# A transformer layer's feed-forward network in parts of 8, 8 and 6 blocks, the down projection of two parts wholly in seven products

## The chip, the cores and the metric

The kernel runs on one core of one Trainium2 chip. The metric is the device time of one execution in microseconds (us), from runs of the same built kernel. The core's engines are named as in the profile: PE is the tensor engine, DVE the vector engine, ACT the scalar engine, POOL GpSimd, SP the engine that here issues most transfers. Each takes its instructions in the order in which the program lists them; they meet at semaphores.

## What is computed

Two layers work on 512 tokens of width 1024, in float32. Each layer mixes the tokens (attention, convolution, neighbourhood attention, merged by gates), then applies a feed-forward network, then a gated embedding. The change concerns the feed-forward network:

```
h = rmsnorm(x, norm_ffn[i])
x = x + (jax.nn.silu(h @ w_ffn_gate[i]) * (h @ w_ffn_up[i])) @ w_ffn_down[i]
```

The inner width is 2816, so 22 blocks of 128 (`NFB`). "Gate" and "up" give a block of middles, 128 x 512 (inner features by tokens); "down" multiplies all 22 blocks into 8 outputs of 128 x 512.

## The kernel before, in words

**Numbers as pairs.** Every operand of PE is split into a rounded high part and a rest (`split`, line 169): ACT copies the high part (line 150), DVE subtracts it (`tt`, line 164). A product of two operands is then three matmuls: high by high, high by low, low by high.

**Seven products.** Where two blocks of weights and two blocks of tokens form a 2 by 2 arrangement, the kernel computes the four results from seven block products in place of eight, as Strassen and Winograd do. The operands of the seven are sums: of weights (s1 to s4, built by accumulating transfers of POOL and by DVE) and of activations (t1 to t4). A product's moving side is 256 tokens wide.

**Three parts.** `ffn` (line 1244) walks the 22 blocks in three parts (`PARTS`): blocks 0 to 7, 8 to 14 and 15 to 21. For each block, `seven` (line 1129) multiplies the gate and up weights by the normalised tokens in seven products of 12 matmuls; DVE and ACT combine the results, apply silu and the product of gate and up, and split the middle block (`rest`). `rest` of a block is called in the next block, after its third product, by `flush`; after the last block of a part it is called at once. After each part, the down projection of that part's blocks runs:

- Parts one and two use `seven_down` (line 1030), called for p = 0 to 3, each for a pair of outputs (2p, 2p+1). Six blocks, paired as (0,1), (2,3), (4,5), go through the seven products R0, R1, T0, T1, A0, A1, C0. Each takes three chunks k, one for each pair of blocks, so nine matmuls of 128 x 256. The blocks that are left (`late`: 6 and 7 in part one, 14 in part two) are multiplied whole, each by two outputs (steps M and N, lines 1085 to 1087), three matmuls of 128 x 512 a time. The result goes to DRAM (`xa`).
- Part three uses ordinary products: `pair` for outputs 0 and 1, `gemm` for the rest, 7 blocks x 3 matmuls of 128 x 512 (lines 187 to 189) an output. During its blocks, `x[m]` is loaded from `xa[0]` and `xa[1]` is added by accumulating transfers of POOL.

**Sums of middles.** When a pair of middle blocks is ready, `middles` (line 1002) forms t1 to t4: u (t1 and t3 together, 512 columns), w (t2 and t4, 256 columns each), and splits each into high and low. The splits are put off to the `rest` of the next block (`parted`, `part_sums`); for the pair (12,13) the split of t2 comes at once. In an even block that takes part in the seven products only the first 256 columns are split, since its second half enters the products through sums alone.

**Order.** PE's order is that of the code (`manual_schedule`). The order on ACT, DVE and the queues is decided by a scheduler with priorities; work on weights is put ahead (`high_priority`), and `behind` pins one instruction behind another.

## Time and profile before

| what | us |
|---|---|
| median of 3 runs | 1760.77 |
| the runs | 1759.83 to 1761.42 |
| the profiled execution | 1761.55 |
| its span, first to last instruction | 1759.8 |
| layer 1: blocks 0 to 7 end, part one's down projection starts | 573.67 |
| part two's blocks start | 614.87 |
| part two's down projection starts | 685.19 |
| part three's blocks start | 721.17 |
| part three's down projection, start and end | 791.45, 829.56 |

Times are counted from the first instruction. A row of the timeline gives start, duration, engine, line, operation, output and inputs, shape. Rows of PE start before the row ahead has ended, since matmuls are pipelined: the distance of two starts is what a matmul costs. The same holds in a small way on DVE and ACT: the distance of starts counts where an engine has no pause.

### The profile page before, as it was taken

The page shows a single profiled execution, that of the slowest core. Times are in us where ns is not written, and L with a number is a line of the kernel's source. Part 1 is how long each engine was busy: PE and PEld are TensorE (multiplying, and loading weights), DVE is VectorE, ACT ScalarE, POOL GpSimd, SP SyncE. Part 2 cuts the span into 40 slices and gives each one's busy share as a digit, 9 for nine tenths or more (in the row PEclk, how much of TensorE's full clock was granted, in tenths as well). Part 3 has the DMA queues.
Part 4 walks back from the last instruction along what each step waited for, and adds up shares of the span by engine and source line. Part 5 has one row for each costly group of instructions (what it writes and reads, how often), then busy time and mean ns, then how long its engine had stood idle before and what let it go on. Part 6 is the DMA issues. An engine that isn't in the chain of part 4 may idle for free.

```text
span 1759.8 us, 28716 instructions
## 1 busy us (share of the span) xinstructions
PE 1752.0 (100%) x10578; PEld 1565.5 (89%) x10578; DVE 1473.8 (84%) x2528; ACT 929.6 (53%) x1623; POOL 140.3 (8%) x162
## 2 busy tenths in 40 slices
PE   9999999999999999999999999999999999999998
PEld 7888888888899999998888888888888999999987
DVE  7967987998799889887777678889887997998776
ACT  5576545225576455554545655552356654555454
POOL 0000000000111111210000000000001121112100
PEclk9999999999999999999999999999999999999999
DMA  6576641334867777975446755423257667779642
GB/s 225 165 186 160 162 126 45 111 99 141 265 167 173 205 194 171 253 206 165 159 134 175 180 148 152 113 72 96 93 173 245 178 167 218 187 189 253 159 153 96
DMA packets 137901, 288.67 MB, mean 164 GB/s; under 512 B 17184, under 2 KB 38432, under 8 KB 137760
## 3 DMA queue, kind: packets, MB, share of 16 engines
q1 hardware_dynamic: 117456, 251.96, 46.6%
q0 software_dynamic: 19584, 33.56, 12.0%
q8 instruction: 83, 1.36, 0.3%
q10 hardware_dynamic: 720, 1.31, 0.2%
q14 instruction: 58, 0.48, 0.1%
HBM read 236.43 MB, written 19.92 MB: 146 GB/s over the span
## 4 chain that ended last, share of the span: by engine, by line
PE 92%; DVE 4%; ACT 2%; DMA 1%; issue 1%; SPq 0%; POOL 0%; ACTq 0%; POOLq 0%; DVEq 0%
PE ffn_mm L1174 4%; PE ffn_mm L1176 4%; PE ffn_mm L1175 4%; PE ffn_sc L1174 3%; PE ffn_sc L1176 3%; PE ffn_sc L1175 3%; PE mergea_mm L188 2%; PE mergea_mm L189 2%; PE mergea_mm L187 2%; PE gateb_mm L188 2%; PE gateb_mm L189 2%; PE gateb_mm L187 2%; PE wo_mm L187 2%; PE wo_mm L189 2%; PE wo_mm L188 2%; PE diff_sc L837 2%
## 5 line engine op out<-in xcount | busy, mean ns | idle before, releaser
L167 DVE SCALAR_TENSOR_TENSOR conv_z<-glu_z,pre_par,conv_z 128x512 f32<-128x512 f32 x240 | 179.4, 748 | 3.5
L1144 POOL DMA_DIRECT2D ffn_qk<-w_fu x88 | 77.8, 973 | 432.8 <-DMA ffn_qk<-w_fu 88.7
L164 DVE TENSOR_TENSOR ffn_wl<-ffn_wr,ffn_wh 128x1024 fp32r<-128x1024 f32 (+1 forms) x76 | 89.3, 1177 | 6.7 <-ACT ffn_wh L150 6.7
L150 ACT ACTIVATE ffn_wh<-ffn_qk 128x1024 fp32r<-128x1024 f32 (+1 forms) x60 | 62.7, 1045 | 51.8 <-PE ffn_mm L1087 14.6
L150 ACT ACTIVATE ffn_wh<-ffn_wr 128x1024 fp32r<-128x1024 f32 (+1 forms) x76 | 76.8, 1014 | 22.5 <-PE ffn_mm L188 12.0
L150 ACT ACTIVATE mergea_wh<-mergea_wr 128x1024 fp32r<-128x1024 f32 (+1 forms) x32 | 27.1, 846 | 96.8 <-PE mergea_mm L188 79.6
L164 DVE TENSOR_TENSOR ffn_wl<-ffn_qk,ffn_wh 128x1024 fp32r<-128x1024 f32 (+1 forms) x60 | 72.3, 1205 | 6.7 <-ACT ffn_wh L150 6.3
L150 ACT ACTIVATE ffn_kh<-ffn_r 128x512 fp32r<-128x512 f32 (+1 forms) x60 | 35.9, 599 | 42.0 <-PE ffn_mm L1175 19.9
L233 POOL TENSOR_TENSOR diff_rc<-diff_sm,pre_power 128x4 f32<-128x4 f32 x8 | 8.9, 1116 | 563.8 <-DVE diff_sm L167 505.3
L150 ACT ACTIVATE diff_a<-diff_sc,diff_s 128x512 f32<-128x512 f32 x32 | 22.0, 686 | 57.2 <-DVE diff_s L931 57.1
L150 ACT ACTIVATE natten_e<-natten_e,natten_s 128x192 f32<-128x192 f32 (+1 forms) x88 | 39.3, 473 | 24.0 <-DVE natten_s L735 20.7
L1174 PE MATMUL ffn_sc<-wo_h,ffn_wh 128*128 128x256 f32 x176 | 50.4, 286 | 0.2 <-ACT ffn_t L150 0.2
L1175 PE MATMUL ffn_mm<-wo_h,ffn_wh 128*128 128x256 f32 x176 | 49.8, 283 | 0.0
L1176 PE MATMUL ffn_mm<-wo_h,ffn_wl 128*128 128x256 f32 x176 | 49.8, 283 | 0.0
L1174 PE MATMUL ffn_mm<-wo_h,ffn_wh 128*128 128x256 f32 x176 | 49.8, 283 | 0.0
L1176 PE MATMUL ffn_sc<-wo_h,ffn_wl 128*128 128x256 f32 x176 | 49.8, 283 | 0.0
L1175 PE MATMUL ffn_sc<-wo_h,ffn_wh 128*128 128x256 f32 x176 | 49.8, 283 | 0.0
L164 DVE TENSOR_TENSOR diff_wl<-diff_wr,diff_wh 128x1024 fp32r<-128x1024 f32 x24 | 29.3, 1223 | 18.6 <-ACT diff_wh L150 13.6
L150 ACT ACTIVATE natten_wh<-natten_wr 128x1024 fp32r<-128x1024 f32 x24 | 25.4, 1059 | 36.7 <-issue 15.2
L931 DVE TENSOR_REDUCE diff_s<-diff_sc 128x1 f32<-128x512 f32 x64 | 42.0, 683 | 2.7 <-PE diff_sc L837 2.5
L164 DVE TENSOR_TENSOR natten_wl<-natten_wr,natten_wh 128x1024 fp32r<-128x1024 f32 x24 | 29.3, 1222 | 12.4 <-ACT natten_wh L150 10.4
L164 DVE TENSOR_TENSOR ffn_qk<-ffn_qk,ffn_r 128x512 f32<-128x512 f32 (+1 forms) x60 | 38.9, 648 | 0.0
(1082 smaller groups left out, 6979.5 us busy)
## 6 DMA issues: line engine op xcount, KB each, us to landing
ffn_qk<-w_fu POOLq DMA_DIRECT2D x88, 256.0 KB, 6.5
ffn_wr<-w_fg SPq DMA_DIRECT2D x44, 512.0 KB, 5.5
ffn_r<-w_fu SPq DMA_DIRECT2D x44, 256.0 KB, 4.6
ffn_qk<-w_fg SPq DMA_DIRECT2D x44, 256.0 KB, 4.8
ffn_qk<-w_fu SPq DMA_DIRECT2D x44, 256.0 KB, 5.2
...
```

The source lines that it names most:

```text
L150: i = self.nc.scalar.activation(out, in_, func, **kw)
L164: return self.nc.vector.tensor_tensor(out, a, b, op)
L167: return self.nc.vector.scalar_tensor_tensor(out, a, s, b, op0, op1)
L187: mm(out, wh, ah, start=first, stop=False, skip_group_check=onto)
L188: mm(out, wh, al, start=False, stop=False, skip_group_check=onto)
L189: mm(out, wl, ah, start=False, stop=last, skip_group_check=onto)
L837: self.nc.tensor.matmul(out, st4[:, u, qs], st[:, ks], start=n == 0, stop=n == 1)
L931: nc.vector.tensor_reduce(out=m[:, u:u + 1], in_=sc, op=ALU.max, axis=AX.X, negate=True)
L1144: nc.gpsimd.dma_start(q, wu[:, lo], accum_op=ALU.add)
L1174: mm(out, wh[:, c], bh, start=first and k == 0, stop=False, skip_group_check=True)
L1175: mm(out, wh[:, c], bl, start=False, stop=False, skip_group_check=True)
L1176: mm(out, wl[:, c], bh, start=False, stop=k == 3, skip_group_check=True)
```

## The change

- `PARTS` becomes 0 to 7, 8 to 15 and 16 to 21. In parts one and two all eight blocks go through the seven products (four chunks, `KW` of 512), steps M and N are gone, and `DOWN`, the order in which the weights of the down projection lie in DRAM, follows. Part three has six blocks an output.
- Blocks 6 and 7 (14 and 15) get sums too (`middles` with `last`): their splits are not put off, and come in the order t2, t1, t3, then t4. In block 6 (14) only 256 columns are split.
- For p = 0 the seven products run in two rounds: first chunks 0 to 2 of all seven, then chunk 3, which holds the last two blocks, in the order R0, A0, A1, T0, R1, T1, C0 (`ORDERS`). For p = 1 the order is R0, A0, T0, A1, R1, T1, C0, for p = 2 and 3 it is `STEPS`.
- On the queues: a call of `seven_down` loads two sums of 256 KB, one block of 512 KB and one of 256 KB through SP (before: sums of 192 KB and a remainder, a block of up to 512 KB, and 192 KB), and POOL adds two of 256 KB (before 192 KB). The loads of `x` from `xa` move one block later.
- Two orders are pinned: for p = 1 the high part of the sums s1, s2 behind t4's low part, and p = 0's first subtraction behind p = 1's sum s4.

The diff, cut to its core:

```diff
-PARTS = (range(0, 8), range(8, 15), range(15, 22))
+PARTS = (range(0, 8), range(8, 16), range(16, 22))
...
-KW = 3 * P
-DOWN = (0, 2, 4, 1, 3, 5, 6, 7, 8, 10, 12, 9, 11, 13, *range(14, NFB))
+KW = 4 * P
+ORDERS = {0: ("R0", "A0", "A1", "T0", "R1", "T1", "C0"), 1: ("R0", "A0", "T0", "A1", "R1", "T1", "C0")}
+STEPS = ("R0", "A0", "R1", "T1", "T0", "A1", "C0")
+DOWN = (*range(0, 8, 2), *range(1, 8, 2), *range(8, 16, 2), *range(9, 16, 2), *range(16, NFB))
 QUARTERS = (2, 4, 6)
 ORDER = (0, 2, 4, 6, 1, 3, 5, 7)
...
@@ -167,7 +169,7 @@
         return self.nc.vector.scalar_tensor_tensor(out, a, s, b, op0, op1)
 
     def split(self, hi, lo, src):
-        self.act(hi, src, AF.Copy)
+        self.high = self.act(hi, src, AF.Copy)
         return self.tt(lo, src, hi.bitcast(F32), ALU.subtract)
 
...
         two, (t2, t4) = at
+        t1, t3 = [(t[:, :256], t[:, 256:]) for t in (two if last else (two[:, 0], two[:, 1]))]
 
         def four():
...
-                  lambda: self.split(*t2, w[:, 0]), lambda: self.split(*t4, w[:, 1])]
         if last:
...
+                self.split(hi, lo, t)
+            four()
+            self.four_low = self.split(*t4, w[:, 1])
         else:
             four()
-        self.parted += parted
-        return dict(t1=(two[:, 0, :256], two[:, 0, 256:]), t3=(two[:, 1, :256], two[:, 1, 256:]),
-                    t2=t2, t4=t4)
+            self.parted += [lambda: self.split(two[:, :, :256], two[:, :, 256:], u),
+                            lambda: self.split(*t2, w[:, 0]), lambda: self.split(*t4, w[:, 1])]
+        return dict(t1=t1, t2=t2, t3=t3, t4=t4)
 
     def part_sums(self):
 
...
-    def seven_down(self, p, w0, w1, bs, late, spare, last):
+    def seven_down(self, p, w0, w1, bs, spare, to):
...
-            n = 2 * KW + len(late) * P
-            one, two, end = slice(0, KW), slice(KW, 2 * KW), slice(2 * KW, n)
+            one, two = slice(0, KW), slice(KW, 2 * KW)
...
             nc.sync.dma_start(sums[:, one], w0[:, one])
             nc.sync.dma_start(sums[:, two], w1[:, two])
-            nc.sync.dma_start(sums[:, end], w1[:, end])
-            nc.sync.dma_start(g[:, :n], w0[:, :n])
+            nc.sync.dma_start(g, w0)
             nc.sync.dma_start(a22, w1[:, two])
             for q in (one, two):
                 nc.gpsimd.dma_start(sums[:, q], w1[:, one], accum_op=ALU.add)
...
-            halve(*wide(), g[:, :n], ("a11", "a12", "m0"))
+            halve(*wide(), g, ("a11", "a12"))
             low = halve(self.sb("kh", [P, 512], F32R), self.sb("a", [P, 512], F32R), a22, ("a22",))
-            if last and p == 1:
-                self.behind(low, self.held)
-            halve(*wide(), sums[:, :n], ("s1", "s2", "m1"))
+            halve(*wide(), sums, ("s1", "s2"))
+            if p == 1:
+                self.behind(self.high, self.four_low)
             self.behind(self.tt(more[:, one], sums[:, one], a22, ALU.add), low)
-            self.tt(more[:, two], more[:, one], g[:, two], ALU.add)
-            halve(*spare, more[:, :2 * KW], ("s3", "s4"))
-        tags = (("tr", "tr", "mm", "mm"), ("sc", "sc", *(("mm", "av"), ("av", "mm"))[last]))[(p + last) % 2]
+            i = self.tt(more[:, two], more[:, one], g[:, two], ALU.add)
+            if p == 1:
+                self.behind(self.later_q, i)
+            halve(*spare, more, ("s3", "s4"))
+        tags = (("tr", "tr", "mm", "mm"), ("sc", "sc", "mm", "av"))[p % 2]
         R, T, A, C = (self.ps(t, (P, 2, 256)) for t in tags)
...
+        used, left = set(), {n: 4 for n in STEPS}
+
+        def product(step, ks):
...
+            first = step[0] not in used
+            used.add(step[0])
+            left[step] -= len(ks)
...
-            for k in range(3):
+            for k in ks:
                 c = slice(k * P, k * P + P)
                 bh, bl = bs[k][b]
-                mm(out, wh[:, c], bh, start=first and k == 0, stop=False, skip_group_check=True)
+                mm(out, wh[:, c], bh, start=first and k == ks[0], stop=False, skip_group_check=True)
                 mm(out, wh[:, c], bl, start=False, stop=False, skip_group_check=True)
-                mm(out, wl[:, c], bh, start=False, stop=k == 2, skip_group_check=True)
-            self.chunk2()
...
-        def whole(out, w, k, first):
...
-            mm = nc.tensor.matmul
-            out = out.rearrange("p a b -> p (a b)")
-            mm(out, wh[:, c], bh, start=first, stop=False, skip_group_check=True)
-            mm(out, wl[:, c], bh, start=False, stop=False, skip_group_check=True)
-            mm(out, wh[:, c], bl, start=False, stop=True, skip_group_check=True)
...
-        order = "R0 T0 R1 T1 A0 M N A1 C0"
+                mm(out, wl[:, c], bh, start=False, stop=k == 3, skip_group_check=True)
+            if k == 3:
+                self.chunk2()
+
         if p == 0:
-            order = ("R0 T0 R1 T1 A0 A1 MN C0", "R0 A0 T0 R1 T1 A1 MN C0")[last]
-        elif last and p == 1:
-            order = "R0 A0 M R1 T1 N T0 A1 C0"
-        elif last:
-            order = "R0 A0 R1 T1 T0 M N A1 C0"
+            for step in STEPS[:2] + ("T0", "R1", "T1", "A1", "C0"):
+                product(step, (0, 1, 2))
...
-        used, done = [], set()
-        for step in order.split():
-            if step in steps:
-                out, u, w, b = steps[step]
-                product(out[:, u], w, b, id(out) not in used)
-                used.append(id(out))
...
-            done.add(step)
-            if e0 is None and {"R0", "R1"} <= done:
+        for step in ORDERS.get(p, STEPS):
+            product(step, (3,) if p == 0 else (0, 1, 2, 3))
+            if e0 is None and not left["R0"] + left["R1"]:
                 e0 = self.sb("t", [P, 2, 256])
                 i = self.act(e0, R, AF.Copy)
-                if last and p == 0:
+                if p == 0:
                     self.behind(i, self.held)
...
-                q = self.sb("a", [P, 256])
+            if e1 is None and e0 is not None and not left["T0"] + left["T1"]:
+                q = self.sb("a" if p else "ss", [P, 256])
...
+                self.later_q = self.tt(q, T[:, 0], e0[:, 0], ALU.subtract)
...
-            self.tt(e, out, e, ALU.add)
-            nc.sync.dma_start(self.xa[last][2 * p + m], e.rearrange("p a b -> p (a b)"))
+            u = slice(0, 2 - m)
+            self.tt(e[:, u], out[:, u], e[:, u], ALU.add)
+            nc.sync.dma_start(to[2 * p + m], e.rearrange("p a b -> p (a b)"))
...
-            n = 256 if fb in (0, 2, 4, 8, 10, 12) else 512
+            n = 256 if fb < 16 and fb % 2 == 0 else 512
...
+        xt.append([self.sb("e", [P, 512], F32R) for _ in range(2)])
...
-                for m in {16: (0, 1), 17: (2, 3), 18: (4, 5), 19: (6, 7)}.get(fb, ()):
+                for m in {17: (0, 1), 18: (2, 3), 19: (4, 5), 20: (6, 7)}.get(fb, ()):
                     self.behind(nc.sync.dma_start(x[m], self.xa[0][m]), self.held)
-                for m in {17: (0, 1), 18: (2, 3), 19: (4, 5), 20: (6, 7)}.get(fb, ()):
+                for m in {18: (0, 1), 19: (2, 3), 20: (4, 5), 21: (6, 7)}.get(fb, ()):
                     self.behind(nc.gpsimd.dma_start(x[m], self.xa[1][m], accum_op=ALU.add), self.held)
...
-                gg = xg[:, fb % 2].rearrange("p (a b) -> p a b", a=2) if f < 6 and fb < 14 else None
+                gg = xg[:, fb % 2].rearrange("p (a b) -> p a b", a=2) if fb < 16 else None
...
-                    if f > 5 or fb > 13 or fb % 2 == 0:
+                    if fb > 15 or fb % 2 == 0:
...
-                    free = [cut(self.halves(t), two) for t in (*h[::2], md8[0], md8[2])][f - 1:f + 1]
+                    free = [cut(self.halves(t), two) for t in (*h[::2], *md8[:7:2])][f - 1:f + 1]
                     low.append(dict(b11=cut(ha, one), b21=cut(hb, one), b22=cut(hb, two),
-                                    **self.middles((xt[f // 2], free), xg, fb == 13)))
...
-                    w0, w1 = (self.a["w_fd"][i, 2 * p + u][:, part[0] * P:] for u in range(2))
-                    self.seven_down(p, w0, w1, low, mids[6:], spare[(p + n) % 2], n)
+                    w0, w1 = (self.a["w_fd"][i, 2 * p + u][:, part[0] * P:(part[0] + 8) * P] for u in range(2))
+                    self.seven_down(p, w0, w1, low, spare[p % 2], self.xa[n])
```

Two places show how the change moves instructions. The first is DVE at the end of part one, in layer 1. Before, after the splits of the weights for p = 0 (`ffn_wl_5886`, `ffn_pt_4771`) and the first one for p = 1 (`ffn_wl_5994`) come block 6's product of gate and up (`ffn_t_5624<-ffn_t_5624,ffn_t_5625`) and block 7's seven steps (from `ffn_a_5757` to the scaling `ffn_t_5758<-ffn_t_5758,wo_rb_4910`, after which ACT applies silu):

```order
L164 TENSOR_TENSOR ffn_pt_4771<-ffn_qk_4788,ffn_pt_4770 128x768
L164 TENSOR_TENSOR ffn_wl_5994<-ffn_wr_5984,ffn_wh_5993 128x1024
L164 TENSOR_TENSOR ffn_t_5624<-ffn_t_5624,ffn_t_5625 128x512
L164 TENSOR_TENSOR ffn_v_4776<-ffn_t_5670,ffn_v_4776 128x256
L164 TENSOR_TENSOR ffn_a_5757<-ffn_t_5756,ffn_a_5757 128x256
L164 TENSOR_TENSOR ffn_t_5758<-ffn_sc_5753,wo_rb_4910 128x256
L164 TENSOR_TENSOR ffn_y_4780<-ffn_t_5624,ffn_y_4780 128x512
L164 TENSOR_TENSOR ffn_t_5756<-ffn_sc_5753,ffn_t_5756 128x256
L164 TENSOR_TENSOR ffn_t_5759<-ffn_t_5756,ffn_av_5755 128x256
L164 TENSOR_TENSOR ffn_t_5758<-ffn_sc_5754,ffn_t_5756 128x256
L164 TENSOR_TENSOR ffn_t_5759<-ffn_t_5759,ffn_a_5757 128x256
L164 TENSOR_TENSOR ffn_t_5758<-ffn_t_5758,wo_rb_4910 128x256
```

In the changed kernel (`tt` is line 166 there) the four further steps on the weights for p = 1 (`ffn_a_6018`, `ffn_qk_4790<-ffn_qk_4789,ffn_r_6006`, `ffn_qk_4790<-ffn_qk_4790,ffn_wr_6005`, `ffn_y_4773`) stand here too; block 6's product of gate and up is `ffn_x_4785<-ffn_x_4785,ffn_t_5626`, and block 7's seven steps begin with `ffn_a_5758`:

```order
L166 TENSOR_TENSOR ffn_a_6018<-ffn_r_6006,ffn_kh_6017 128x512
L166 TENSOR_TENSOR ffn_pt_4771<-ffn_qk_4790,ffn_pt_4770 128x1024
L166 TENSOR_TENSOR ffn_wl_6014<-ffn_wr_6005,ffn_wh_6013 128x1024
L166 TENSOR_TENSOR ffn_qk_4790<-ffn_qk_4789,ffn_r_6006 128x512
L166 TENSOR_TENSOR ffn_x_4785<-ffn_x_4785,wo_rb_4912 128x256
L166 TENSOR_TENSOR ffn_qk_4790<-ffn_qk_4790,ffn_wr_6005 128x512
L166 TENSOR_TENSOR ffn_v_4774<-ffn_t_5671,ffn_v_4774 128x256
L166 TENSOR_TENSOR ffn_x_4785<-ffn_x_4785,ffn_t_5626 128x512
L166 TENSOR_TENSOR ffn_v_4776<-ffn_t_5671,ffn_v_4776 128x256
L166 TENSOR_TENSOR ffn_y_4773<-ffn_qk_4790,ffn_y_4772 128x1024
L166 TENSOR_TENSOR ffn_y_4780<-ffn_x_4785,ffn_y_4780 128x256
L166 TENSOR_TENSOR ffn_a_5758<-ffn_t_5757,ffn_a_5758 128x256
```

So the splits and sums of p = 1's weights, which stood behind block 7's steps, now stand ahead of them. After the last of the seven steps (`ffn_x_4785<-ffn_x_4785,wo_rb_4912`) follow block 7's product of gate and up, the sum u (`ffn_t_5868`), block 7's low part (`ffn_e_4782`), w, and the low parts of t1, t3 (`ffn_e_4787`, `ffn_e_4788`) and t2 (`ffn_y_4778`), then t4's sum:

```order
L166 TENSOR_TENSOR ffn_x_4785<-ffn_x_4785,wo_rb_4912 128x256
L166 TENSOR_TENSOR ffn_x_4785<-ffn_x_4785,ffn_t_5759 128x512
L166 TENSOR_TENSOR ffn_t_5868<-ffn_x_4785 128x512
L166 TENSOR_TENSOR ffn_e_4782<-ffn_x_4785,ffn_e_4781 128x512
L166 TENSOR_TENSOR ffn_t_5869<-ffn_x_4785,ffn_t_5868 128x256
L166 TENSOR_TENSOR ffn_e_4787<-ffn_t_5868,ffn_e_4787 128x256
L166 TENSOR_TENSOR ffn_e_4788<-ffn_t_5868,ffn_e_4788 128x256
L166 TENSOR_TENSOR ffn_y_4778<-ffn_t_5869,ffn_y_4778 128x256
L166 TENSOR_TENSOR ffn_t_5869<-ffn_x_4785,ffn_t_5869 128x256
```

The same rows, with other numbers, stand at the end of part two, and of both parts in layer 2.

The second place is PE in the first call of `seven_down`. Before, its last steps are the whole products of blocks 6 (`ffn_y_4780`) and 7 (`ffn_e_4781` high, `ffn_e_4782` low):

```order
L1087 MATMUL ffn_mm_5895<-ffn_y_4780,ffn_wh_5877 128x512
L1085 MATMUL ffn_mm_5896<-ffn_y_4780,ffn_wh_5885 128x512
L1086 MATMUL ffn_mm_5896<-ffn_y_4780,ffn_wl_5886 128x512
L1087 MATMUL ffn_mm_5896<-ffn_y_4780,ffn_wh_5885 128x512
L1085 MATMUL ffn_mm_5895<-ffn_e_4781,ffn_wh_5877 128x512
L1086 MATMUL ffn_mm_5895<-ffn_e_4781,ffn_wl_5878 128x512
L1087 MATMUL ffn_mm_5895<-ffn_e_4782,ffn_wh_5877 128x512
L1085 MATMUL ffn_mm_5896<-ffn_e_4781,ffn_wh_5885 128x512
L1086 MATMUL ffn_mm_5896<-ffn_e_4781,ffn_wl_5886 128x512
L1087 MATMUL ffn_mm_5896<-ffn_e_4782,ffn_wh_5885 128x512
```

In the changed kernel, after the first round (its last matmul is `ffn_mm_5908<-ffn_v_4776,ffn_a_5894`), chunk 3 of R0, A0 and A1 reads block 6 and then block 7, and T0 reads t2 (`ffn_y_4778`):

```order
L1086 MATMUL ffn_mm_5908<-ffn_v_4776,ffn_a_5894 128x256
L1084 MATMUL ffn_tr_5905<-ffn_y_4780,ffn_wh_5889 128x256
L1085 MATMUL ffn_tr_5905<-ffn_y_4780,ffn_wh_5889 128x256
L1086 MATMUL ffn_tr_5905<-ffn_y_4780,ffn_wl_5890 128x256
L1084 MATMUL ffn_mm_5907<-ffn_e_4781,ffn_wh_5889 128x256
L1085 MATMUL ffn_mm_5907<-ffn_e_4782,ffn_wh_5889 128x256
L1086 MATMUL ffn_mm_5907<-ffn_e_4781,ffn_wl_5890 128x256
L1084 MATMUL ffn_mm_5907<-ffn_e_4781,ffn_pt_4770 128x256
L1085 MATMUL ffn_mm_5907<-ffn_e_4782,ffn_pt_4770 128x256
L1086 MATMUL ffn_mm_5907<-ffn_e_4781,ffn_pt_4771 128x256
L1084 MATMUL ffn_tr_5906<-ffn_y_4778,ffn_pt_4770 128x256
```

Block 7 is now read in the fourth matmul behind the first round, in products 256 wide.

29 lines of the change are left out of this document (8 added, 21 removed).

## The prediction

> **What bounds the kernel now.** I read the page's shares first, then the windows of the three down projections of layer 1, then the timeline of PE, DVE and ACT where part one's down projection starts. The page:
>
> ```profile
> span 1759.8 us, 28716 instructions
> PE 1752.0 (100%) x10578; PEld 1565.5 (89%) x10578; DVE 1473.8 (84%) x2528; ACT 929.6 (53%) x1623; POOL 140.3 (8%) x162
> ```
>
> PE is never long without work, so time falls where matmuls go and rises where PE is made to wait. But 84% for DVE is a mean. The windows show the last block of part one (first row) and then the three down projections; the columns are length, then busy time and count of PE, weight loads, DVE, ACT, POOL, then granted clock, DMA share and GB/s:
>
> ```profile
> core 0: us, PE busy (x) PEld busy (x) DVE busy (x) ACT busy (x) POOL busy (x), PEclk, DMA share, GB/s
> 563.59:573.67 10.08, 10.08 (x86) 10.08 (x85) 10.04 (x20) 6.59 (x12) 1.72 (x2) 1.00 0.70 165
> 573.67:614.87 41.20, 41.20 (x302) 39.24 (x301) 33.23 (x58) 17.05 (x22) 7.05 (x8) 1.00 0.76 200
> 685.19:721.17 35.98, 35.98 (x278) 34.63 (x277) 30.73 (x58) 15.88 (x22) 7.03 (x8) 1.00 0.86 229
> 791.45:829.56 38.11, 38.11 (x170) 31.54 (x169) 28.26 (x42) 18.37 (x27) 0.00 (x0) 1.00 0.52 163
> ```
>
> In the last block of a part DVE is busy for 10.04 of 10.08 us: there are two bounds at once, and whatever is put into DVE's queue there comes out later by its whole length. In the down projections DVE has 5 to 10 us to spare. Part one's down projection begins so on PE:
>
> ```profile
> 573.67 0.28 PE L1074 MATMUL ffn_tr<-ffn_v,ffn_wh 128*128 128x256 f32 x1
> 573.79 0.28 PE L1075 MATMUL ffn_tr<-ffn_v,ffn_wh 128*128 128x256 f32 x1
> ...
> 581.99 0.39 PE L1087 MATMUL ffn_mm<-ffn_e,ffn_wh 128*128 128x512 f32 x1
> ```
>
> A matmul of 256 columns costs 0.12 us. The last row is the first reader of block 7's low part, 8.3 us after the start. Now DVE and ACT around it:
>
> ```profile
> 566.26 0.41 DVE L164 TENSOR_TENSOR ffn_t<-ffn_mm,wo_rb 128x256 f32<-128x256 f32 x1
> ...
> 567.26 0.68 DVE L164 TENSOR_TENSOR ffn_x<-ffn_t,ffn_x 128x512 fp32r<-128x512 f32 x1
> 567.86 0.41 DVE L164 TENSOR_TENSOR ffn_t<-ffn_t,ffn_mm 128x256 f32<-128x256 f32 x1
> 568.19 0.41 DVE L164 TENSOR_TENSOR ffn_t<-ffn_mm,ffn_t 128x256 f32<-128x256 f32 x1
> 568.52 0.55 DVE L164 TENSOR_TENSOR ffn_a<-ffn_r,ffn_kh 128x384 fp32r<-128x384 f32 x1
> 568.99 0.55 DVE L164 TENSOR_TENSOR ffn_qk<-ffn_qk,ffn_r 128x384 f32<-128x384 f32 x1
> ...
> 572.94 1.21 DVE L164 TENSOR_TENSOR ffn_wl<-ffn_wr,ffn_wh 128x1024 fp32r<-128x1024 f32 x1
> 574.07 0.68 DVE L164 TENSOR_TENSOR ffn_t<-ffn_t,ffn_t 128x512 f32<-128x512 f32 x1
> ...
> 577.73 0.42 DVE L164 TENSOR_TENSOR ffn_t<-ffn_t,wo_rb 128x256 f32<-128x256 f32 x1
> ...
> 580.94 0.69 DVE L164 TENSOR_TENSOR ffn_e<-ffn_t,ffn_e 128x512 fp32r<-128x512 f32 x1
> ```
>
> ```profile
> 578.18 0.63 ACT L150 ACTIVATE ffn_t<-ffn_t 128x512 f32<-128x512 f32 x1 [0.47 <-DVE ffn_t L164]
> 580.26 0.63 ACT L150 ACTIVATE ffn_e<-ffn_t 128x512 fp32r<-128x512 f32 x1 [1.44 <-DVE ffn_t L164]
> ```
>
> Distances of starts give DVE's price by columns: 0.33 us for 256, 0.47 for 384, 0.60 for 512, 1.13 for 1024, and so about 0.87 for 768. Block 7's last scaling ends at 578.15, silu follows after 0.03, its high part starts at 580.26, and its low part ends at 581.63: 0.36 before PE reads it. The cover is nearly used up already.
>
> **The matmuls.** Per layer, part one had 4 calls of 63 matmuls of 256 and 12 of 512. 252 x 0.12 = 30.24 of the window's 41.20, so 48 of 512 took 10.96, or 0.228 each. The changed part has 4 x 84 of 256: 336 x 0.12 = 40.32, that is -0.88. Part two had 252 x 0.12 + 24 x 0.228 = 35.71, and its window has 0.27 more, which I take for a wait that goes with the whole products; now 40.32, or +4.34. Part three had 168 in 38.11, 0.227 each; now 144, 32.67, or -5.44. Together -1.98 a layer, -3.96 in all. Two rounds in place of one for p = 0 issue the same matmuls and cost nothing by themselves: PE passes from one product to the next at 0.12 too.
>
> [...]
>
> **The end of part one.** The order shows DVE's rows unchanged up to block 6's scaling (566.26). From there to the end of block 7's last scaling, the changed queue has p = 1's low part of a22, its sums s3 and s4 (512 columns each) and the low part of those (1024) in front, 3 x 0.60 + 1.13 = 2.93 more. p = 0's a22, s3 and s4 grow from 384 to 512 (3 x 0.13 = 0.39), the low part of its s3 and s4 from 768 to 1024 (0.26), and block 6's low part shrinks from 512 to 256 (-0.27). Sum +3.31: block 7's scaling ends at 581.46 in place of 578.15. DVE is full, so nothing in front absorbs the 3.31. Nor do p = 1's transfers hold it up, of which a22 is issued last:
>
> ```profile
> 559.27 0.33 SPq L1043 DMA_DIRECT2D ffn_r<-w_fd  x1
> ```
>
> ```profile
> ffn_r<-w_fd SPq DMA_DIRECT2D x3, 192.0 KB, 3.0
> ```
>
> It lands about 562.3, 9 us ahead of its new place in DVE's queue (571.8).
>
> Then the chain, with 0.03 from DVE to ACT (577.73 + 0.42 to 578.18) and 0.05 back (580.26 + 0.63 to 580.94): silu 581.49 to 582.12, product of gate and up 582.17 to 582.86, high part 582.89 to 583.52, low part 583.57 to 584.26. PE's first round takes 63 x 0.12 = 7.56 and ends at 581.23; R0's chunk 3 needs block 6 alone, and ends at 581.59. A0 then wants block 7's high part and gets it at 583.57: PE waits **1.98**. Its second matmul wants the low part, due 583.69, there at 584.31: **0.62**. A0 ends at 584.55, A1 at 584.91. DVE goes on with w (584.17 to about 584.59), two low parts of 256, and t2's low part (585.16 to 585.58), while ACT makes t2's high part by 585.03. T0 waits **0.17** for the one and **0.43** for the other, and ends at 585.87; R1 and T1 follow to 586.59. t4's sum (585.49), high part and low part end at 586.83, so C0 waits **0.17**, and the call ends at 587.12, not at 583.75: **3.37** of waiting. p = 1 then has its first four products' weights ready; its R1 comes 5.8 us later, more than the some 2.4 that two parts of 1024 columns take (1.21 on DVE, taken to be alike on ACT). No further wait.
>
> **The end of part two** has the same rows in the same order. Its place against PE:
>
> ```profile
> 647.21 0.41 DVE L164 TENSOR_TENSOR ffn_x<-ffn_mm,wo_rb 128x256 f32<-128x256 f32 x1
> ...
> 667.32 0.42 DVE L164 TENSOR_TENSOR ffn_x<-ffn_mm,wo_rb 128x256 f32<-128x256 f32 x1
> ```
>
> ```profile
> 675.15 0.28 PE L1174 MATMUL ffn_mm<-wo_h,ffn_wh 128*128 128x256 f32 x1
> ...
> 685.19 0.28 PE L1074 MATMUL ffn_sc<-ffn_v,ffn_wh 128*128 128x256 f32 x1
> ```
>
> A pair of blocks takes DVE 20.11 us and PE 2 x 10.04. Block 12's scaling (667.32) comes 7.83 before block 13's end (675.15); block 14's will come 7.80 before block 15's, where block 6's came 7.41 before 573.67. DVE is 0.39 further ahead, so the first wait is 1.59 and the sum **2.98**.
>
> **Part three** loses cover too. Before, 36 matmuls (six blocks of two outputs, 8.2 us at 0.227) ran ahead of the first that reads block 21:
>
> ```profile
> 791.45 0.40 PE L187 MATMUL ffn_mm<-ffn_v,ffn_wh 128*128 128x512 f32 x1
> ```
>
> ```profile
> 795.17 0.69 DVE L164 TENSOR_TENSOR ffn_y<-ffn_t,ffn_y 128x512 fp32r<-128x512 f32 x1 [0.70 <-ACT ffn_y L150]
> ```
>
> The block was whole at 795.86, 4.4 us after the start and 3.8 early; with 30 matmuls (6.8 us) it is still 2.4 early: nothing. The loads of x move one block later on SP and POOL, two blocks behind the end of part two as before: nothing, with a bound of 0.3 a block if they push a weight's sum late. The larger weight transfers, 1792 KB a call (SP and POOL) in 10.08 us against 1472 KB in 9.0, would take DMA's share from 0.86 to about 0.93 in part two: below full, so nothing, and at most a few tenths.
>
> **Sum.** Per layer -1.98 + 3.37 + 2.98 = +4.37; in all +8.7. The profiled execution's 1761.55 (span 1759.8 and 1.8 around it) becomes 1770.3; against the median of the runs, 0.8 lower, **1769.5**. Its own range is 1767 to 1773: half a microsecond either way on each of four waits, and a few tenths of transfers.
>
> **Rivals.** *Hidden* (the other side): the first round covers block 7 and its sums, all waits are nothing, and -3.96 remains: 1756.8. It needs DVE 2.0 us further ahead in part one and 1.6 in part two. For it: 7.92 us of matmuls lie ahead of A0's chunk 3, not far from the 8.3 that the old order gave block 7. Against it: DVE's 10.04 of 10.08, and a chain that had 0.36 to spare with less in front of it.
>
> *First wait only*: A0 waits, but the sums follow behind it without more loss, since PE's queue or ACT bridges the tenths: 2 x (1.98 + 1.59) - 3.96 = +3.2, 1764.0. Against it, DVE is in sequence behind the low part.
>
> *Clock*: after a wait of 2 us PE resumes slowly. The trace's first matmuls show such a state:
>
> ```profile
> 1.06 3.78 PE L338 MATMUL pre_av<-pre_zeror 128*128 128x512 f32 x8 [1.06 <-DVE pre_zeror L411]
> 4.64 0.63 PE L383 MATMUL pre_mm<-glu_v,pre_y 128*128 128x512 f32 x1
> ```
>
> Eight of 512 take the 3.58 us to the next row, 0.45 each, twice the 0.228 above. Such a stretch after each wait loses 1.8 us, four of them 7.2: 1776.7. No wait in these windows, with clock 1.00, is long enough to test it.
>
> [...]
>
> **Numbers.** Forecast 0.74, first wait only 0.12, hidden 0.07, clock 0.04, others 0.03. 0.2% (3.5 us) is about what a measurement of this kernel can tell from no change: below 1757.2 is faster, above 1764.3 slower. Hidden lies on the lower edge (0.05 faster, 0.02 same), first wait only on the upper one (0.08 same, 0.04 slower): 0.05 faster, 0.11 same, 0.84 slower with the rest. The range reaches from the middle of *first wait only* to the forecast's upper end: 1763.5 to 1773.5.
>
> **What would show it.** In the changed profile: down projections of about 43.7, 43.3 and 32.7 us; a gap of 2 us on PE ahead of the fourth matmul of the second round, put down to ACT's high part of `ffn_e`; block 7's scaling ending some 7.8 us after the round's start; rows for p = 1's weights before it on DVE. I am wrong if that gap is missing, if DVE reaches block 6's scaling earlier than 7.4 us before the part's end, or if PE waits at p = 1 or in part three.

## The result and the profile after

| | median, us | runs |
|---|---|---|
| before | 1760.85 | 6 (1759.83 to 1761.47) |
| changed | 1775.8 | 6 (1775.17 to 1776.88) |

The ratio is 1.0086, with a 95% interval of 1.0073 to 1.0099. The change costs 14.95 us, where 8.7 were forecast, and the time lies 2.3 us above the range. The page of the changed kernel begins so:

```profile
span 1774.2 us, 29007 instructions
PE 1756.2 (99%) x10722; PEld 1574.3 (89%) x10722; DVE 1492.3 (84%) x2556; ACT 941.0 (53%) x1639; POOL 140.9 (8%) x162
```

PE now has 18.0 us of the span without work (1774.2 - 1756.2), where it had 7.8. The windows say where: the down projections of the three parts of layer 1, then those of layer 2, with the columns of the windows shown in the prediction:

```profile
573.11:617.88 44.77, 42.60 (x338) 41.93 (x337) 36.68 (x64) 19.18 (x26) 7.02 (x8) 0.96 0.75 202
698.25:743.36 45.11, 42.83 (x338) 42.10 (x337) 36.61 (x64) 19.17 (x26) 7.02 (x8) 0.96 0.77 204
803.85:836.52 32.67, 32.67 (x146) 27.04 (x145) 26.60 (x40) 17.04 (x26) 0.00 (x0) 1.00 0.58 180
1452.47:1497.64 45.17, 42.83 (x339) 42.09 (x337) 36.62 (x64) 19.17 (x26) 7.05 (x8) 0.96 0.72 194
1578.03:1621.81 43.78, 41.50 (x339) 40.65 (x338) 36.53 (x64) 19.18 (x26) 7.02 (x8) 1.00 0.77 209
1682.05:1714.71 32.66, 32.66 (x146) 27.03 (x145) 26.58 (x40) 17.04 (x26) 0.00 (x0) 1.00 0.57 179
```

Part three takes 32.7 us, as forecast. Parts one and two were to take 43.7 and 43.3; they take 43.78 to 45.17, and the three that take over 44.7 are those with a granted clock of 0.96. PE in layer 1, part one, where the second round passes from R0 to A0:

```profile
580.95 0.28 PE L1086 MATMUL ffn_tr<-ffn_y,ffn_wl 128*128 128x256 f32 x1
583.06 0.39 PE L1084 MATMUL ffn_mm<-ffn_e,ffn_wh 128*128 128x256 f32 x1 [1.83 <-ACT ffn_e L152]
583.78 0.39 PE L1085 MATMUL ffn_mm<-ffn_e,ffn_wh 128*128 128x256 f32 x1 [0.34 <-DVE ffn_e L166]
```

From one start to the next 2.11 and 0.72 us pass in place of 0.12: waits of 1.99 and 0.60, where 1.98 and 0.62 were forecast, put down to the instructions that were named. The waits came as forecast. What follows them did not. Narrower windows around this place show the clock (third column from the end):

```profile
580.95:584.24 3.29, 1.12 (x8) 0.72 (x6) 2.56 (x5) 2.12 (x5) 0.00 (x0) 1.00 0.73 125
584.24:587.64 3.40, 3.40 (x17) 3.12 (x15) 1.93 (x6) 1.74 (x4) 0.00 (x0) 0.50 0.00 0
587.64:592.00 4.36, 4.36 (x38) 4.36 (x38) 4.21 (x8) 3.03 (x4) 0.00 (x0) 1.00 0.34 95
```

For 3.40 us the granted clock is 0.50. The counts of PE, 17 and 38, take in every matmul that reaches into the window: 14 start in these 3.40 us, 37 in the 4.36 us after them. PE waits in the stretch for only some 0.4 us, at T0; from 585.50 on its matmuls follow at 0.213 us in place of 0.12. Such a stretch lies in three of the four places, not in the fourth (1578.03).

A third loss lies behind part three, at the transposes for the norm, in both layers (here layer 1):

```profile
841.74 0.39 PE L191 MATMUL ple_mm<-ffn_qk,ple_wl 128*128 128x512 f32 x1
842.90 0.66 PE L225 MATMUL ffn_tr<-pre_ident,ffn_ss 128*128 128x128 f32 x4 [0.78 <-DVE ffn_ss L166]
```

1.16 us lie between starts that are usually 0.23 apart: 0.93 of waiting for the last sum of squares. Before, PE did not wait there:

```profile
834.77 0.40 PE L189 MATMUL ple_mm<-ffn_qk,ple_wl 128*128 128x512 f32 x1
835.01 0.60 PE L223 MATMUL ffn_tr<-pre_ident,ffn_ss 128*128 128x128 f32 x4
```

The chain to it in the changed kernel, first on ACT, then on DVE:

```profile
836.54 1.06 ACT L152 ACTIVATE ple_wh<-ple_wr 128x1024 fp32r<-128x1024 f32 x1 [1.89 <-issue]
837.51 0.71 ACT L152 ACTIVATE ffn_z<-ffn_x,pre_par 128x512 fp32r<-128x512 f32 x1
```

```profile
837.64 1.23 DVE L166 TENSOR_TENSOR ple_wl<-ple_wr,ple_wh 128x1024 fp32r<-128x1024 f32 x1 [0.26 <-ACT ple_wh L152]
838.78 0.75 DVE L169 SCALAR_TENSOR_TENSOR ffn_z<-ffn_x,pre_par,ffn_z 128x512 fp32r<-128x512 f32 x1
839.44 0.69 DVE L166 TENSOR_TENSOR ffn_ss<-ffn_ss,ffn_t 128x512 f32<-128x512 f32 x1
840.04 0.69 DVE L166 TENSOR_TENSOR ffn_t<-ffn_mm,wo_rb 128x512 f32<-128x512 f32 x1
...
842.15 0.69 DVE L166 TENSOR_TENSOR ffn_ss<-ffn_ss,ffn_t 128x512 f32<-128x512 f32 x1 [0.63 <-ACT ffn_t L152]
```

The last output's last matmul starts at 836.29 and the next product begins at 836.52, but DVE turns to the output at 840.04, 3.52 us after that. Ahead of it stand the low part of the third ple weight (`ple_wl`, for the gated embedding that follows), the low part of output 6 as scaled for the norm, and its sum of squares. `ple_wl` needs ACT's `ple_wh`, in front of which ACT had been idle for 1.89 us. The profile names no releaser for that; `ple_wh` starts 0.02 us after PE's part three ends, which fits a buffer that PE frees with it. Before, the order on DVE was another:

```profile
830.40 0.68 DVE L164 TENSOR_TENSOR ffn_t<-ffn_mm,wo_rb 128x512 f32<-128x512 f32 x1
831.00 1.21 DVE L164 TENSOR_TENSOR ple_wl<-ple_wr,ple_wh 128x1024 fp32r<-128x1024 f32 x1
```

The last output, which PE had ended at 829.56, came 0.84 us later and ahead of the ple weight.

The account of the 14.4 us between the two spans, from windows and rows of the same work:

| | forecast | measured |
|---|---|---|
| matmuls (40.36, 40.36 and 32.66 a layer where nothing waits, against 41.20, 35.98 and 38.11) | -4.0 | -3.8 |
| waits in parts one and two: 4 x (43.78 - 40.36) | 12.7 | 13.7 |
| half rate: 44.77, 45.11 and 45.17, less 43.78 each | 0 | 3.7 |
| norm behind part three, 0.93 and 0.94 | 0 | 1.9 |
| everything else | 0 | -1.1 |
| sum | 8.7 | 14.4 |

The 40.36 is from an experiment below. Of the last line, -0.56 lies ahead of part one of layer 1 and -0.90 between the layers; these were not followed further.

### The profile page after: what moved, and what is told of

It is laid out like the page before. It is cut to its first block, busy times and chain, and to the rows that moved or that the text cites. A ratio compares the mean times of both kernels' runs of the same rounds, so it can differ in the third digit from the quotient of the medians.

```text
span 1774.2 us, 29007 instructions
## 1 busy us (share of the span) xinstructions
PE 1756.2 (99%) x10722; PEld 1574.3 (89%) x10722; DVE 1492.3 (84%) x2556; ACT 941.0 (53%) x1639; POOL 140.9 (8%) x162
## 3 DMA queue, kind: packets, MB, share of 16 engines
q0 software_dynamic: 19584, 35.66, 12.7%
## 4 chain that ended last, share of the span: by engine, by line
PE 86%; DVE 10%; issue 2%; ACT 1%; DMA 1%; POOL 0%; ACTq 0%; POOLq 0%; DVEq 0%; SPq 0%
PE ffn_mm L1158 3%; PE ffn_mm L1160 3%; PE ffn_mm L1159 3%; PE mergea_mm L190 2%; PE mergea_mm L191 2%; PE mergea_mm L189 2%; PE ffn_sc L1158 2%; PE ffn_sc L1159 2%; PE ffn_sc L1160 2%; PE diff_sc L839 2%; PE diff_mm L189 2%; PE diff_mm L191 2%; PE diff_mm L190 2%; PE gatec_mm L190 2%; PE gatec_mm L191 2%
## 5 line engine op out<-in xcount | busy, mean ns | idle before, releaser
L152 ACT ACTIVATE ffn_wh<-ffn_qk 128x1024 fp32r<-128x1024 f32 x60 | 63.5, 1059 | 40.2 <-PE ffn_sc L1159 12.2
L166 DVE TENSOR_TENSOR ffn_wl<-ffn_qk,ffn_wh 128x1024 fp32r<-128x1024 f32 x60 | 73.4, 1224 | 10.0 <-ACT ffn_wh L152 9.4
L152 ACT ACTIVATE ffn_kh<-ffn_r 128x512 fp32r<-128x512 f32 x60 | 37.7, 628 | 61.5 <-PE ffn_mm L1159 15.7
L166 DVE TENSOR_TENSOR ffn_qk<-ffn_qk,ffn_r 128x512 f32<-128x512 f32 x60 | 41.1, 685 | 0.0
L166 DVE TENSOR_TENSOR ffn_qk<-ffn_qk,ffn_wr 128x512 f32<-128x512 f32 x60 | 41.1, 685 | 0.0
```

The source lines that it names most:

```text
L152: i = self.nc.scalar.activation(out, in_, func, **kw)
L166: return self.nc.vector.tensor_tensor(out, a, b, op)
```

## The experiments

The theory, "queue": the weights of p = 1, ahead of block 7's chain on DVE, make block 7 late; the two rounds do not cover it; idle time of PE then brings the half rate, which costs extra; and the wait at the norm is a matter of its own. The rival, "shape": eight-chunk sums by seven products, in two rounds, cost PE something by themselves.

**The queue of DVE put right** (e1_order). The weights of p = 1 go behind t4's low part, and p = 1 takes its products in the order of the others:

```diff
+            if p == 1:
+                self.behind(low, self.four_low)
             halve(*wide(), sums, ("s1", "s2"))
...
-            if p == 1:
-                self.behind(self.later_q, i)
...
-ORDERS = {0: ("R0", "A0", "A1", "T0", "R1", "T1", "C0"), 1: ("R0", "A0", "T0", "A1", "R1", "T1", "C0")}
+ORDERS = {0: ("R0", "A0", "A1", "T0", "R1", "T1", "C0")}
```

> p = 1's a22, s3 and s4 are put behind t4's low part on DVE, in both parts, so that 2.93 us of weights no longer stand ahead of block 7's chain; the changed kernel's 1775.8 us is the base. Queue theory (the waits at A0, its low part and T0 come from what stands ahead of block 7 on DVE): A0's high part comes about 2.9 us earlier than the 583.06 of the changed kernel, at 580.1, before PE asks for it at 580.95 to 581.1; the waits of 3.0 to 3.3 us at each of four places shrink to under 0.5 each, the half-rate stretches behind them go too, and the time is 1775.8 - 12 - 4.6 = about 1759, with up to 2 more if p = 1 now waits for its own late weights. Shape theory (two rounds and eight-chunk sums cost PE something by themselves): still 1770 or more.

Measured: 1761.92 us, ratio to before 1.0008 (1.0000 to 1.0017). ACT's row for block 7's high part, then PE at T0:

```profile
579.87 0.64 ACT L152 ACTIVATE ffn_e<-ffn_x 128x512 fp32r<-128x512 f32 x1 [0.76 <-DVE ffn_x L166]
```

```profile
582.21 0.28 PE L1084 MATMUL ffn_tr<-ffn_y,ffn_pt 128*128 128x256 f32 x1
582.62 0.39 PE L1085 MATMUL ffn_tr<-ffn_y,ffn_pt 128*128 128x256 f32 x1
```

In the changed kernel that row stood at 582.38, 9.27 us after the start of the round (573.11); here it is 6.30 after it (573.57). It comes 2.97 us sooner, for 2.93 us of DVE's work moved out of the way. A0 does not wait, nor does p = 1 for its later weights; 0.29 us at T0 is the longest wait left in the window. The queue theory holds, the shape theory falls. That 1759 wasn't reached is these small waits: the windows take 41.12 us, not 40.36.

**The cover made longer** (e2_cover). DVE's queue is left alone; the first round of p = 1, as far as its weight buffers allow, comes between the two rounds of p = 0:

```diff
-        if p == 0:
-            for step in STEPS[:2] + ("T0", "R1", "T1", "A1", "C0"):
+        if p < 2:
+            for step in (("R0", "A0", "T0", "R1", "T1", "A1", "C0"), ("R0", "A0", "T0", "A1", "C0"))[p]:
                 product(step, (0, 1, 2))
+            yield
...
-            product(step, (3,) if p == 0 else (0, 1, 2, 3))
+            product(step, range(4 - left[step], 4))
...
-                    self.seven_down(p, w0, w1, low, spare[p % 2], self.xa[n])
+                    g = self.seven_down(p, w0, w1, low, spare[p % 2], self.xa[n])
+                    if p == 0:
+                        first = g
+                    for q in ((g,), (g, first, g), (g,), (g,))[p]:
+                        next(q, None)
```

> DVE's queue stays row for row as in the changed kernel; on PE, 45 matmuls of p = 1 (chunks 0 to 2 of R0, A0, T0, A1, C0) are put between p = 0's first and second round, 45 x 0.12 = 5.4 us of cover, and R1, T1 of p = 1 go last. Queue theory: block 7's high part still comes at about 583.0 and t4's low part at about 586.8, but PE asks 5.4 us later (586.5), so all waits of 3.0 to 3.3 us at each of four places go, and with them the half-rate stretches (three of about 1.5 us): 1775.8 - 12.4 - 4.6 = about 1759. Shape theory: still 1770 or more. If p = 1's weights (s3, s4) come too late for the earlier place, a new wait ahead of its T0, up to 2 us each, 1767.

Measured: 1762.04 us, ratio 1.0010 (1.0001 to 1.0019). Block 7's high part on ACT, then PE at A0 and later in p = 2:

```profile
582.54 0.63 ACT L152 ACTIVATE ffn_e<-ffn_x 128x512 fp32r<-128x512 f32 x1 [0.76 <-DVE ffn_x L166]
```

```profile
586.52 0.28 PE L1086 MATMUL ffn_tr<-ffn_y,ffn_wl 128*128 128x256 f32 x1
586.64 0.28 PE L1084 MATMUL ffn_mm<-ffn_e,ffn_wh 128*128 128x256 f32 x1
...
599.36 0.28 PE L1085 MATMUL ffn_tr<-wo_h,ffn_pt 128*128 128x256 f32 x1
600.28 0.38 PE L1086 MATMUL ffn_tr<-wo_h,ffn_pt 128*128 128x256 f32 x1 [0.64 <-DVE ffn_pt L166]
```

Block 7 is as late as in the changed kernel, but PE asks for it only at 586.64, 3.5 us after it is there, and goes on at 0.12. The old wait is gone and a smaller new one stands in p = 2: 0.80 us at T0, four times, for the low part of s3 and s4. They use the buffer that p = 0 held, and p = 0 now ends 5.4 us later. The next run takes this wait away.

**C0 ahead of T0 in p = 2** (e6_cover_c0), one line more:

```diff
+          2: ("R0", "A0", "R1", "T1", "C0", "T0", "A1")}
```

> As the run with cover (1762.0 us), but p = 2 takes C0 ahead of T0. Queue theory: the one wait that the cover left behind, 0.80 us four times at p = 2's T0 for the low part of its s3 and s4 (their buffer comes free 5.4 us later than before), gets 12 x 0.12 = 1.44 us more and goes: 1762.0 - 3.2 = 1758.8. Shape theory (eight-chunk sums cost something by themselves): at 1762.

Measured: 1759.36 us, ratio 0.9993 (0.9984 to 1.0002). Parts one and two of layer 1:

```profile
573.84:614.19 40.35, 40.35 (x338) 40.35 (x337) 36.16 (x64) 19.15 (x26) 7.00 (x8) 1.00 0.78 210
694.57:734.93 40.36, 40.36 (x338) 40.36 (x337) 36.10 (x64) 19.15 (x26) 7.04 (x8) 1.00 0.83 225
```

This is 336 matmuls of 0.12, with no wait and the clock at 1.00, for the prediction's 40.32. Eight-chunk sums cost nothing beyond their matmuls.

**One round** (e8_one_round): p = 0's products run whole, in the order R0, A0, A1, T0, R1, T1, C0.

```diff
-        if p == 0:
-            for step in STEPS[:2] + ("T0", "R1", "T1", "A1", "C0"):
-                product(step, (0, 1, 2))
...
-            product(step, (3,) if p == 0 else (0, 1, 2, 3))
+            product(step, (0, 1, 2, 3))
```

> The two rounds of p = 0 are undone, its seven products run whole in the order R0, A0, A1, T0, R1, T1, C0. Queue theory: A0's chunk 3 is asked for after 21 matmuls (2.5 us, at 575.7), not after 66, but block 7's high part still comes at about 583.0, so the first wait grows from 1.99 to about 7.3 and the later ones nearly go (0.6 left for the low part): 8.0 in place of 3.2 at each of four places, +19, and after so long a wait the half rate in all four: 1775.8 + 19 + 1.4 = about 1796. Shape theory (two rounds cost more than they cover): less than 1785.

Measured, in a single run: 1797.21 us. The time is as expected, but not its split:

```profile
573.70 0.28 PE L1086 MATMUL ffn_tr<-ffn_y,ffn_wl 128*128 128x256 f32 x1
576.83 0.38 PE L1084 MATMUL ffn_tr<-ffn_y,ffn_wh 128*128 128x256 f32 x1 [2.86 <-ACT ffn_y L152]
578.12 0.58 PE L1085 MATMUL ffn_tr<-ffn_y,ffn_wh 128*128 128x256 f32 x1 [0.91 <-DVE ffn_y L166]
...
580.43 0.41 PE L1086 MATMUL ffn_mm<-ffn_y,ffn_wl 128*128 128x256 f32 x1
582.69 0.58 PE L1084 MATMUL ffn_mm<-ffn_e,ffn_wh 128*128 128x256 f32 x1 [1.85 <-ACT ffn_e L152]
```

R0's chunk 3 already waits, 3.01 and 1.17 us, for block 6, which I had thought long ready; A0 waits 2.14 more. And the granted clock is 0.50 for 10.24 us in each of the four places, three times 3.41 (its mean over the execution is 0.988). So the first round of the change covers block 6 as well, and is worth about 21 us here, half rate included. It is too short, not useless.

**The waits filled** (e3_fill). PE works through them on matmuls that go to an unused half of C's bank:

```diff
+        def fill(n):
+            for _ in range(n):
+                nc.tensor.matmul(C[:, 1], ws["a11"][0][:, :P], bs[0]["b11"][0], start=False, stop=False,
+                                 skip_group_check=True)
...
+                if p == 0 and k == 3:
+                    fill({"A0": 16, "T0": 4}.get(step, 0))
                 mm(out, wh[:, c], bh, start=first and k == ks[0], stop=False, skip_group_check=True)
+                if p == 0 and k == 3:
+                    fill({"A0": 5}.get(step, 0))
```

> The waits stay, but PE runs 25 matmuls of 256 columns in them whose sums nobody reads: 16 ahead of A0's chunk 3, 4 behind its first matmul, 5 ahead of T0 (16 x 0.12 = 1.92 of 1.99, 0.48 of 0.60, 0.60 of 0.60). Clock theory (the 0.213 us per matmul after the waits is half rate, set off by PE's idle time): the stretches at 0.213 go, PE stays at 0.120, and the time falls by what they cost, three of about 1.5 us: 1771.2. Rival (the slow stretch comes from something else that happens at that time, transfers or PSUM): the matmuls there stay at 0.213, and the time stays at 1775.8 or rises.

(As built, 5 stand behind A0's first matmul and 4 ahead of T0, not 4 and 5.)

Measured: 1772.98 us, 2.8 less than the changed kernel by doing more. Two of its four windows:

```profile
573.05:616.89 43.84, 43.84 (x363) 43.53 (x362) 36.59 (x64) 19.19 (x26) 6.96 (x8) 1.00 0.75 198
1450.15:1494.00 43.85, 43.85 (x363) 43.52 (x362) 36.52 (x64) 19.19 (x26) 7.04 (x8) 1.00 0.76 204
```

All four windows take 43.79 to 43.85 us, with the clock at 1.00. The transfers, the buffers and the real work are those of the changed kernel. Where the waits were left whole (the changed kernel, e5_norm and e9_norm_pin below) seven of twelve places have the half rate, here none of four. The mean granted clock on record says the same of the other executions: 0.999 to 1.000 in all five here, 0.997 in all six of the changed kernel. So the half rate goes with PE's idle time. It costs 1.0 to 1.4 us a place, rather than the 1.5 that I had put in.

**Half of the first wait filled** (e4_half): only 8 such matmuls, ahead of A0. Against the run with all waits filled:

```diff
-                    fill({"A0": 16, "T0": 4}.get(step, 0))
+                    fill({"A0": 8, "T0": 0}.get(step, 0))
...
-                    fill({"A0": 5}.get(step, 0))
+                    fill({"A0": 0}.get(step, 0))
```

> Only 8 matmuls whose sums nobody reads, ahead of A0's chunk 3: 0.96 of the first wait of 1.99 is filled, 1.0 + 0.6 + 0.6 of waiting stays at each of four places. If the half rate needs one idle stretch of near 2 us, it goes and the time is that of the run with all waits filled, 1773.0; if it comes from the sum of the waits or from their being split up, some of the four places still show 0.213 us a matmul, and the time is 1773 to 1776.

Measured: 1775.64 us (1774.03 to 1777.24). In the profiled execution one place of four has the half rate:

```profile
573.86:617.70 43.84, 42.44 (x346) 41.60 (x345) 36.61 (x64) 19.18 (x26) 7.04 (x8) 1.00 0.74 194
1451.73:1496.90 45.17, 43.79 (x347) 43.06 (x346) 36.64 (x64) 19.17 (x26) 7.06 (x8) 0.96 0.73 189
```

The same waits, about 1.0, 0.60 and 0.44 us, stand in both rows. No single wait near 2 us is needed, and one and the same pattern of waits does and does not bring it.

**Only the first wait left** (e10_tail): the 1.99 us stay whole, the two shorter waits are filled, with 5 matmuls and 4. Against the run with all waits filled:

```diff
-                    fill({"A0": 16, "T0": 4}.get(step, 0))
+                    fill({"A0": 0, "T0": 4}.get(step, 0))
```

> The first wait of 1.99 us at A0 stays whole at each of four places; the two shorter ones behind it (0.60 and about 0.60) are filled with 4 and 5 matmuls whose sums nobody reads. If one wait of 2 us is enough for the half rate, three of the four places show 0.213 us a matmul as in the changed kernel, and the time stays at 1775.8. If it is the sum of the waits that does it (3.2 in 4.2 us in the changed kernel; with 2.1 in 4 us one place of four still showed it), about one place shows it, 1774; none, 1773.

Measured: 1775.12 us, from 1772.93 to 1778.74 in five runs. The lowest is the profiled one, and no place of it has the half rate (windows of 43.79 to 43.86 us, clock 1.00). The spread of 5.8 us is about four times 1.4, as if zero to four places had it in one execution or another. The mean granted clock on record bears that out: it goes from 0.999 (1772.93 and 1774.61 us) to 0.996 (1778.74 us), and four stretches of 3.41 us at half rate would take 0.004 from it. This run doesn't tell one wait from the sum of the waits.

**Where the half rate falls.** The traces at hand tell more; no run was made to test it. In the changed kernel the clock falls at 584.23, 710.53 and 1464.87, each time for 3.41 us (3.413 in the trace's record of the clock), and once more behind the last matmul, at 1772.07. The later three lie 126.30, 880.64 and 1187.84 us behind the first, 37, 258 and 348 times 3.413: in this execution the falls lie on a raster of 3.413 us, a row of evenly spaced times. Here are the raster's stretch ahead of the fall at 710.53 and the stretch of that fall, then the two stretches of the same raster over the waits of the fourth place, where none came:

```profile
707.11:710.53 3.42, 1.86 (x9) 1.33 (x10) 3.36 (x8) 1.77 (x4) 0.00 (x0) 1.00 0.11 19
710.53:713.94 3.41, 3.41 (x18) 3.41 (x17) 2.17 (x4) 2.90 (x5) 0.00 (x0) 0.50 0.49 156
1584.34:1587.75 3.41, 1.82 (x16) 1.61 (x14) 2.65 (x7) 1.14 (x2) 0.00 (x0) 1.00 0.88 146
1587.75:1591.17 3.42, 2.74 (x16) 2.15 (x16) 2.94 (x8) 1.97 (x6) 0.00 (x0) 1.00 0.07 13
```

The waiting within one stretch, that is the distances of PE's starts less 0.12 each, is 2.37 us ahead of this fall, and 2.69 and 2.30 ahead of those at 584.23 and 1464.87; it is 1.75 and 1.51 at the fourth place, where the raster's edge cuts the same waits in two. The changed kernel, e4_half, e5_norm and e9_norm_pin have eight places with a fall and eight without. The stretch ahead of a fall holds 2.06 to 2.69 us of waiting, and the fullest one at a place without a fall 1.92. So in these sixteen places the sum of the waits in one stretch tells the two kinds apart.

**The norm's transposes two steps later** (e5_norm):

```diff
-        self.main_norm(st[0])
+        self.main_norm(st[0], (4, 2))
         return hn
```

> Only the transposes of the norm behind part three are moved two steps (six matmuls of 512, 1.37 us) later on PE. Theory that the shorter part three leaves DVE late there (PE waits 1.07 in each layer for the last sum of squares): both waits go, -2.1 us, 1773.7, with the waits of parts one and two unchanged. Rival (the wait is made good anyway by slack later, or the later transposes delay the row factor that the next product's scaling needs): 1775.8 or above.

Measured: 1781.51 us, 5.7 worse. The edit did more than was expected of it: two steps are two whole products, so that 48 matmuls in place of 24 lie between part three and the transposes, 5.4 us and not 1.37. PE no longer waits at these transposes. Those of the row factor, which follow as far behind as before, come 5.4 us later too, and behind them PE waits for DVE's first scaling of a product by it:

```profile
852.86 0.60 PE L239 MATMUL ffn_tr<-pre_ident,ffn_rc 128*128 128x128 f32 x4
855.85 0.50 PE L189 MATMUL ple_mm<-ffn_qk,ple_wh 128*128 128x512 f32 x1 [2.39 <-DVE ple_t L166]
```

DVE, in the same run:

```profile
853.97 1.22 DVE L166 TENSOR_TENSOR ple_wl<-ple_wr,ple_wh 128x1024 fp32r<-128x1024 f32 x1 [3.44 <-ACT ple_wh L152]
855.11 1.28 DVE L166 TENSOR_TENSOR ple_t<-ple_mm,ffn_rb 128x512 f32<-128x512 f32 x2
```

The scaling (`ple_t`) comes behind the late row factor and behind one more weight split that waits for ACT. In layer 2 the same wait brings a half rate too (1735.39, 3.41 us). So 5.4 us is too late; whether the six matmuls that were meant would have done wasn't tried. The next run makes the norm's input earlier instead.

**The third ple weight behind the norm's squares** (e9_norm_pin). `self.high` and `self.low` are the two halves of the last weight split, `sq` the last square on ACT and its sum on DVE:

```diff
-            self.act(q, x, AF.Square)
-            self.tt(st[0], st[0], q, ALU.add)
+            self.sq = self.act(q, x, AF.Square), self.tt(st[0], st[0], q, ALU.add)
...
-        hn, st = [], []
+        hn, st, sq = [], [], self.sq
...
                 self.gemm(pg, self.a["w_pg"][i, m], h)
+            if m == 2:
+                self.behind(self.high, sq[0])
+                self.behind(self.low, sq[1])
```

> The changed kernel with only the third ple weight's split put behind the last square on ACT and the last sum of squares on DVE. If the norm's wait of 1.07 us a layer is a cost of its own beside those of parts one and two: 1775.8 - 2.1 to - 2.6 = 1773.2 to 1773.7, with the waits of parts one and two unchanged. If the gain seen with it (2.6 us) needed the cover in parts one and two: at 1775.8.

Measured: 1773.93 us, 1.9 below the changed kernel. The norm's wait is gone, the waits of part one (1.99, 0.60, 0.43) stand as they were, and so does part two's first, 1.92: a cost of its own.

**Cover, C0 and the norm together** (e7_cover_c0_norm):

> As the last, and behind part three the split of the third ple weight (wh, wl of m = 2) is put behind the last square on ACT and the last sum of squares on DVE. Theory that ACT, waiting in its queue for a weight buffer that PE frees only with the last output (836.54 in the changed kernel), holds back the scalings and sums of squares of outputs 6 and 7: the transposes of the norm no longer wait (1.07 a layer), 1758.8 - 1.1 (layer 2 alone, if layer 1 makes it good later) to - 2.1, or 1756.7 to 1757.7, which is under the kernel before. Rival (DVE is simply full there, 3.8 of every 4.08 us): the wait stays, 1758.8, or the third ple weight is late and PE waits for it at the third product, up to 1761.

Measured: 1756.74 us, ratio 0.9981 (0.9972 to 0.9990): faster than the kernel before. DVE's last sum of squares, and PE:

```profile
832.26 0.69 DVE L167 TENSOR_TENSOR ffn_ss<-ffn_ss,ffn_t 128x512 f32<-128x512 f32 x1 [0.70 <-ACT ffn_t L153]
```

```profile
833.18 0.39 PE L192 MATMUL ple_mm<-ffn_qk,ple_wl 128*128 128x512 f32 x1
833.41 0.60 PE L226 MATMUL ffn_tr<-pre_ident,ffn_ss 128*128 128x128 f32 x4
```

The transposes follow the matmul at 0.23 us. With every wait of the account gone, 3.65 us of the forecast 3.96 for the matmuls are there (1760.39 - 1756.74).

## Why the prediction was wrong

**The matmuls**: right. 40.36, 40.36 and 32.66 us a layer without waits, against 40.32, 40.32 and 32.67.

**DVE's 3.31 us and the chain behind it**: right. The row that answers to block 7's scaling ends 7.79 us after the round's start in the trace, as worked out (580.48 + 0.42 - 573.11, against 581.46 - 573.67):

```profile
580.48 0.42 DVE L166 TENSOR_TENSOR ffn_x<-ffn_x,wo_rb 128x256 f32<-128x256 f32 x1
```

Two small misses cancel in it: DVE reached block 6's scaling 7.52 us before the part's end (565.59), not 7.41, and needed 3.42 us more from there, not 3.31. The first is one of the prediction's signs of being wrong (earlier than 7.4 us); it came, by some 0.1 us, and did not matter. A0's waits of 1.99 and 0.60 stood for 1.98 and 0.62. T0 came to about 0.6 in both. At C0, in the fourth place, which runs at the full rate, two matmuls come 0.18 us late together, where 0.17 was forecast. That moving 2.93 us out of DVE's queue moves block 7 by 2.97 was shown by e1_order.

**Part two**: slightly low. Its first wait is 1.92 us, not 1.59. DVE was further ahead, as forecast: it reached block 14's scaling 7.82 us before the part's end (690.43 to 698.25), for 7.80. But then it stood:

```profile
695.18 1.23 DVE L166 TENSOR_TENSOR ffn_wl<-ffn_qk,ffn_wh 128x1024 fp32r<-128x1024 f32 x1 [0.26 <-ACT ffn_wh L152]
```

This row starts 0.95 us after the one ahead, of 512 columns, which costs 0.60: 0.35 us of waiting for ACT, and block 15's last scaling ends 7.80 us after the round's start, as in part one. DVE was taken to be full there, and was not. With the tenths behind each wait the four places hold 13.7 us of waiting for a forecast 12.7.

**The clock**: the step that failed most. The sum put it at nothing and the rival *clock* had a chance of 0.04, because no wait before was long enough to test it. It came at three of four places in the profile, for 3.7 us in all. The slow stretch was the rival's; its price of 1.8 a place was too high (1.0 to 1.4), its chance far too low. That its 1776.7 lies only 0.9 us above the measured time is luck: it had four places at too high a price and no wait at the norm. That a wait of 1.98 us with matmuls between would leave the clock alone was my estimate, and no run had shown it. The runs show the opposite: 2.06 to 2.69 us of waiting within one stretch of 3.41 us, in pieces with matmuls between, stood ahead of each of the eight falls in four kernels' profiles.

**"No wait in part three: nothing"**: failed at the end that I had not looked at. I followed its start, where block 21 was early; no wait shows there in the changed kernel. At its end DVE takes the last output behind the ple weight's low part, 3.52 us after PE, where before it took it ahead of that, 0.84 us after; the norm then waits, for 1.9 us in the profile. e9_norm_pin changed the order alone and gave back as much. An output also takes 4.08 us in place of 4.76, which leaves ACT and DVE less time for each; that this made the scheduler choose the other order is not shown.

Without these two the forecast would have been about 5.6 us higher, at 1775. That this comes so near 1775.8 is luck in part: 1.0 us more of waiting in parts one and two stands against 1.1 us less elsewhere, which was not followed.
